# Encoder step on one core: each query tile in one transfer instead of two, differences of the weights ahead of scaling, row tiles normed ahead of stores

## The chip, the cores and the metric

The kernel runs on one core of one Trainium2 chip. The core has five engines with their own instruction streams: TensorE (PE, matmuls), VectorE (DVE), ScalarE (ACT), GpSimd (POOL) and SyncE (SP), which issues most of the DMAs here. Work is passed between them by semaphores. Sixteen DMA engines move the data. The metric is the time of one execution on the device in microseconds (us); a lower one is better.

## The reference, cut to what matters

One step of a two-layer encoder for 2048 prompt frames and 64 new frames (the sample), 16 heads of 64, model width 1024, in float32:

```python
def a_project(x, g, w_in):
    h = rms_norm(x, g)
    q, k, v, gate = jnp.split(h @ w_in, 4, axis=-1)
    return split_heads(q), split_heads(k), split_heads(v), gate
...
def band_attend(q, k, v, q_pos, k_pos, rel_bias):      # layer A: own chunk of 64 and 8 before it
    s = jnp.einsum('bqhd,bkhd->bhqk', q, k).astype(jnp.float32) * SCALE
    ...
    p = jax.nn.softmax(s, axis=-1).astype(v.dtype)
    return jnp.einsum('bhqk,bkhd->bqhd', p, v)
...
def sb_block(q, k, v, q_pos, k_pos):                   # layer B: stick-breaking, 128 queries
    z = jnp.einsum('bqhd,bkhd->bhqk', q, k).astype(jnp.float32) * SCALE
    mask = (k_pos[None, :] < q_pos[:, None])[None, None]
    log_fail = jnp.where(mask, jax.nn.log_sigmoid(-z), 0.0)
    later = jnp.flip(jnp.cumsum(jnp.flip(log_fail, -1), axis=-1), -1) - log_fail
    w = jnp.where(mask, jnp.exp(jax.nn.log_sigmoid(z) + later), 0.0)
    return jnp.einsum('bhqk,bkhd->bqhd', w.astype(v.dtype), v)
```

Layer A: norm, projection to q, k, v and gate, band attention, times SiLU(gate), output projection, residual. Then a shared projection to keys and values, and layer B: norm, projection to q and gate, stick-breaking attention over the shared keys and values, gate, output projection, residual, final norm.

## The kernel before

**Precision and planes.** Each float32 operand of a matmul is split into two parts: a rounded one, made by ACT, and the rest, made by DVE (`split`). The two parts are called planes, and lie beside each other in a tile (`[P, 2, CH]`, P = 128 partitions, CH = 512 frames). A product takes three matmuls.

**Stages on the time axis.** Projections of layer A to about 640 us of the span; band attention 640 to 1262, in two parts by `ORDER`, prompt blocks (1, 0) to 945 and then (3, 2); output projection to 1383; projections of layer B to 1955; stick-breaking attention 1955 to 3093, again in two parts (to 2300 and after it); the end of layer B to 3201. PE and most of the others work in an order that the program writes out; where the program says so (`order.on`), the instructions of the four engines stay in it.

**Scratch.** q, k, v, gates and the attention's outputs go through scratch in device memory, since they don't fit on chip. `lay[L]["q"][hp]` holds the queries of a pair of heads hp, both planes, one plane behind the other (`[2, P, T]`, T = 2112 frames). `put` writes a block of 512 frames of both planes, `load_q` (L1095) reads it for one head (64 of the 128 rows). The first 64 partitions of the tile `q` and the last 64 get the same 64 rows, since each plane of q meets both planes of the keys, which lie above each other in the tile `keys` or `kt`. So `load_q` issues two DMAs, each to 64 partitions, with rows of 2 KB for each plane. A tile q is 512 KB, the pool has three of them, and each item of the attention (one head, one block of 512 queries) uses one. There are 64 items in each layer, 32 in each part. `Queue.load` (L159) and `Queue.store` (L152) put all of these transfers into SP's one queue, which issues them in order. `Sample.queries` reads the 64 frames of the sample in the same scratch.

**Projections.** Each is made for two heads' pairs at a time (function `pair`), for the first 1024 frames (half 0) and then the last 1024 (half 1), in a scheme with seven products instead of eight, which needs sums and differences of blocks of the weights. `weights_of` makes steps for each pair's weights: `load`; `s1` and `s2` scale by the norm's weights (POOL, tile `wraw`, four instructions each); `b1`, `b2` split whole blocks; `-t1` to `-t4` take differences (POOL, `wraw<-wraw`); `t1` to `t4` split these (ACT and DVE, tile `t`). In `pair` the steps of this pair and the two after it (`this`, `following`, `third`) are placed by hand between the products of eight slots. The helper `times` gives three matmuls for each of four blocks; `plain(x)` copies a PSUM bank by ACT (tile `c`).

**Rows.** The values' loop takes row tiles of 128 frames: `fetched` loads one (`xt`), `normed` squares it on ACT (`junk`), makes `rstd` on POOL and scales it there, `turned` transposes it on PE (`ps_tr`), `parted` splits it. `leave()` copies, splits (`vs`, `vn`) and stores the values of a tile, and `tick()` runs waiting steps such as the conversion of the cached values (`vvp`).

Nearly all instructions of PE, ACT, DVE and POOL are recorded under one line, L115, that of the helper which pins the order; they are told apart by the names of their tiles.

Of the kernel before, what the change touches and what calls it, by code (L numbers as in the profile page):

```python
# [78 lines left out]
def f32(ap):  # L79
    return ap.bitcast(F32)  # L80
# [45 lines left out]
def encoder_step(ctx: ExitStack, tc: tile.TileContext, a: dict, o: dict):  # L126
# [73 lines left out]
    for L, rows in (("a", CACHE_A), ("b", PAST)):  # L200
        lay[L] = dict(


            q=[dram.tile([2, P, T], F32R, name=f"q_{L}{i}") for i in range(HP)],
            k=[dram.tile([2, P, T + rows], F32R, name=f"k_{L}{i}") for i in range(HP)],

            v=dram.tile([T + rows, H, P], F32R, name=f"v_{L}"),
            g=[dram.tile([P, T], F32, name=f"gate_{L}{i}") for i in range(HP)],

            o=[dram.tile([HP, P, CH if g < GROUPS else NS], F32, name=f"o_{L}{g}") for g in range(GROUPS + 1)],  # L210

            w={
                x: dram.tile([2, 2, P, 2, 4, P], F32R, name=f"w_{L}{x[0]}{x[1]}")
                for x in DEFER[L] if L in KEPT and x[1] % 2 == 0
            },
        )
# [47 lines left out]

    def put(L, kind, hp, cols, parts, by=nc.sync.dma_start):

        by(f32(lay[L][kind][hp][:, :, cols]).rearrange("s p t -> p s t"), f32(parts))


    def projections(L, x_of, begin, w_v, cv, gv, out_v, jobs, first, prompt, sample, stages):  # L270
        with ExitStack() as own, ExitStack() as beside, ExitStack() as early:
# [9 lines left out]
            def quarter(hf, k0, t0):  # L281
                return [lambda k, i=i: xs[hf][i][:, 4 * k0 + k, t0 * CH : t0 * CH + CH] for i in range(2)]
# [102 lines left out]
            def two_blocks(j, raw, home):  # L385

                out = []
                for i in range(2):
                    k = 2 * j + i
                    h_, l_ = home(k)  # L390
                    act.activation(h_, raw[:, i], AF.Copy, scale=gv[:, k : k + 1])
                    dve.scalar_tensor_tensor(l_, raw[:, i], gv[:, k : k + 1], f32(h_), ALU.mult, ALU.subtract)
                    out.append((h_, l_))
                return out

            def vw(pool):
                return lambda k: [pool.tile([P, CH], F32R, name=f"vw{x}", tag=f"vw{x}{k}", bufs=1) for x in "hl"]
# [132 lines left out]
            def run(does, *names):  # L530
                for x in names:
                    if x in does:
                        does.pop(x)()

            def times(ps, x, w, begin):
                if len(x[0](0).shape) > 2:
                    ps = ps.rearrange("p (r h c) -> p r h c", r=2, h=2)
                for k in range(4):
                    mm(ps, w[0](k), x[0](k), start=(begin and k == 0), stop=False, skip_group_check=True)
                    mm(ps, w[0](k), x[1](k), start=False, stop=False, skip_group_check=True)  # L540
                    mm(ps, w[1](k), x[0](k), start=False, stop=(k == 3), skip_group_check=True)

            def pair(hf, kind, c0, hp, forms, pools, this, following, third, event):
# [11 lines left out]
                def plain(ps):  # L555
                    c = cpool.tile([P, CH], F32, name="c", tag="c", bufs=CS[L])
                    act.activation(c, ps, AF.Copy)
                    return c
# [55 lines left out]
                def lagged():  # L614
                    while lagging:
                        lagging.pop(0)()

                x = psum.tile([P, CH], F32, name="ps_x", tag="mm", bufs=5)
                times(x, quarter(hf, 0, 0), w11, True)
                c1 = plain(x)  # L620
                run(this, "t2", "-t3")
                lagged()
                slot(0)
                z = psum.tile([P, CH], F32, name="ps_z", tag="mm", bufs=5)
# [29 lines left out]
                run(following, "b2")  # L654
                lagged()
                leave(0, 0, c1)
                run(third, "s1")
                slot(6)
                times(x, quarter(hf, 1, 1), t4, False)
                if kind == "k" and hf * HALF + CH - first >= 0:  # L660
                    x = plain(x)
                run(following, "-t2", "-t4")
                lagged()
                leave(0, 1, x)
                slot(7)
# [210 lines left out]
            with tc.tile_pool(name=f"v1_{L}", bufs=1) as pool, tc.tile_pool(name=f"v1s_{L}", bufs=1) as vspool:  # L876
                vps = two_places() if L == "b" else None

                class Strip:
                    def tile(self, shape, dtype, name, tag, bufs):  # L880
                        return opool.tile(shape, dtype, name=name, tag="ol", bufs=2)

                where = [(ahead, 2), (ahead, 2), (ahead, 2), (Strip(), 2), (ahead, 2), (ahead, 2), (pool, 1), (ahead, 2)]
                xt[3] = fetched(seq1[3], *where[3])
                for i, t in enumerate(seq1):
                    leave = values(1, 0, i, t, vws, vspool, vps)
                    tick()
                    if i + 4 < NK:
                        xt[i + 4] = fetched(seq1[i + 4], *where[i + 4])
                    if i + 2 < NK:  # L890
                        parted(seq1[i + 2], turned(seq1[i + 2], xt[i + 2]))
                    if i < 4:
                        values_beside(i, ("oh", "xr"))
                    if i == 5:
                        raw = [block_rows(1, j, ("xr", "xr", "oh", "oh")[j]) for j in range(4)]
                    if i == NK - 1:
                        vws = [x for j in range(4) for x in two_blocks(j, raw[j], vw(ahead if j < 2 else pool))]
                    tick()
                    leave()
                    if i + 3 < NK:  # L900
                        normed(seq1[i + 3], xt[i + 3], ahead)
                    if i == 3:
                        tmp = [opool.tile([P, 2, CH], F32, name="mixed", tag="ol", bufs=2) for _ in range(2)]
                        tmp = [x[:, j] for x in tmp for j in range(2)]
                        mixing = mix(1, 1, tmp)
                    if 3 <= i < NK - 2:
                        mixing.pop(0)()
                    tick()
                for i, t in enumerate(seq1):
                    leave = values(1, 1, i, t, vws, vspool, vps)  # L910
                    tick()
                    tick()
                    leave()
                    if i == 5:
                        run(made[0], "t1")
                    if i == 0:
                        assert not mixing
                        tmp = [ahead.tile([P, 2, CH], F32, name="mixed", tag="xt", bufs=2) for _ in range(2)]
                        tmp = [x[:, j] for x in tmp for j in range(2)]
                        mixing = [x for u in (2, 3, 0) for x in mix(1, u, tmp)]  # L920
                    for _ in range(1 + (i < 3)):
                        if mixing:
                            mixing.pop(0)()
                    if i == 0:
                        raws = [raw_tiles()]
                        new1 = slot(x_new.rearrange("p k t -> p (k t)"))
                        forms = [whole_forms("oh"), None, [new1]]
                        made = [weights_of(*todo[1][0], raws[0], forms)]
                        run(made[0], "load")
                    if i == 2:  # L930
                        run(made[0], "s1")
                    if i == 3:
                        run(made[0], "b1", "s2")
                    if i == 4:
                        run(made[0], "-t1")
                        forms[1] = whole_forms("ol")
                        run(made[0], "b2")
                    if i == 5:
                        assert not mixing
                        run(made[0], "-t2", "-t4")  # L940
                    tick()
                while waiting:
                    tick()
# [151 lines left out]
    def load_q(L, pool, hp, h, q0):  # L1095

        there(L, "q", hp, q0)
        q = pool.tile([P, 2, CH], F32R, name="q", tag="q", bufs=3)
        src = f32(lay[L]["q"][hp][:, h * DH : h * DH + DH, place(q0) : place(q0) + CH]).rearrange("s d t -> d s t")
        for x in range(2):  # L1100
            queue.load(f32(q[x * DH : x * DH + DH]), src)
        return q

    def load_gate(L, pool, hp, q0):
# [27 lines left out]
    class Sample:  # L1132
# [9 lines left out]
        def queries(self, hp):  # L1142
            q = self.q[hp % 3]
            for h in range(2):
                rows = slice(h * DH, h * DH + DH)
                src = f32(lay[self.L]["q"][hp][:, rows, NEW : NEW + NS])
                queue.load(f32(q[rows, :, rows]), src.rearrange("s d t -> d s t"))
            return q

        def gate(self, pool, hp):  # L1150
# [994 lines left out]
```

## Time and profile before

| | us |
|---|---|
| median of 3 runs (lowest, highest) | 3200.28 (3200.26, 3200.92) |
| the profiled execution's own time | 3202.8 |
| its span | 3201.0 |
| PE busy, of the span | 3132.4 |
| DVE, ACT, POOL busy | 2216.5, 1858.9, 1719.1 |
| mean granted PE clock | 0.998 |

The span is the time from the first to the last recorded instruction. Busy time counts only compute instructions. A row of the profile names the engine, the operation, the tile written and the tiles read (out<-in), the shapes, how many, and in brackets how long the engine had been idle before and what ended that. A row of the windows gives for a stretch of the span each engine's busy time and count, then PE's granted clock, the mean busy share of the 16 DMA engines and what they moved.

### The profile page before, as it was taken

How to read it: one execution, taken by the hardware profiler on the slowest of the kernel's cores; microseconds unless marked ns; L12 is line 12 of the kernel's file. 1: busy time of each engine (PE TensorE's matmuls, PEld its weight loads, DVE VectorE, ACT ScalarE, POOL GpSimd, SP SyncE). 2: the span in 40 equal slices, each digit the busy share in tenths (PEclk: the TensorE clock that was granted, in tenths of full speed). 3: DMA queues.
4: the chain of work that ended last, by engine and by line, in shares of the span. 5: the costliest groups of instructions: out<-in, count | busy, mean ns of one | idle time of the engine just before them, and what ended most of it. 6: DMA issues, size and time to landing. Idle time of an engine off the chain costs nothing.

```text
span 3201.0 us, 52147 instructions
## 1 busy us (share of the span) xinstructions
PE 3132.4 (98%) x16784; PEld 2614.5 (82%) x16784; DVE 2216.5 (69%) x3940; ACT 1858.9 (58%) x3743; POOL 1719.1 (54%) x2381
## 2 busy tenths in 40 slices
PE   9999999999999999999999999999999999999999
PEld 7888877778888998877888777888888878888877
DVE  5676466567778775257545664888877888888873
ACT  5444444468888775144544544666666666666652
POOL 3545367636565553035534372444567777777761
PEclk9999999999999999999999999999999999999999
DMA  6598448798899993477998768877644576445423
GB/s 228 199 327 306 170 165 286 247 258 229 227 271 265 250 239 132 155 241 250 324 322 313 269 240 262 234 215 208 191 118 140 155 228 176 115 136 143 133 74 122
DMA packets 476975, 685.28 MB, mean 214 GB/s; under 512 B 61169, under 2 KB 258321, under 8 KB 476702
## 3 DMA queue, kind: packets, MB, share of 16 engines
q1 hardware_dynamic: 474398, 673.56, 68.3%
q10 hardware_dynamic: 2304, 8.39, 0.7%
q8 instruction: 134, 2.20, 0.3%
q14 instruction: 139, 1.14, 0.1%
HBM read 423.06 MB, written 258.76 MB: 213 GB/s over the span
## 4 chain that ended last, share of the span: by engine, by line
PE 71%; DVE 10%; issue 6%; DMA 5%; POOL 4%; ACT 3%; SPq 0%; POOLq 0%; ACTq 0%; DVEq 0%
PE acc L115 11%; PE ps_x L115 10%; PE z L115 10%; PE wt L115 9%; PE ps_o L115 9%; PE ps_j L115 8%; PE ps_v L115 6%; PE ps_z L115 5%; DVE s L115 3%; PE ps_y L115 2%; DVE pl L115 2%; POOL wraw L115 1%; PE ps_q L115 1%; ACT ph L115 1%; DMA wraw<-in_w_in_a 1%
## 5 line engine op out<-in xcount | busy, mean ns | idle before, releaser
L115 DVE TENSOR_TENSOR pl<-wt,ph 128x512 fp32r<-128x512 f32 (+1 forms) x864 | 551.0, 653 | 109.7 <-ACT ph L115 106.0
L115 ACT ACTIVATE ph<-wt 128x512 fp32r<-128x512 f32 (+1 forms) x864 | 484.7, 577 | 191.8 <-PE wt L115 180.5
L115 PE MATMUL wt<-ident,s 128*128 128x128 f32 x3472 | 551.6, 274 | 9.1 <-DVE pl L115 6.4
L115 PEld LDWEIGHTS wt<-ident,s 128*128 128x128 f32 x3472 | 417.6, 141 | 84.2 <-DVE pl L115 13.3
L115 ACT ACTIVATE f<-z 128x512 f32<-128x512 f32 (+4 forms) x680 | 355.1, 536 | 192.5 <-PE z L115 131.7
L115 POOL TENSOR_TENSOR s<-f,s 128x256 f32<-128x256 f32 x416 | 360.3, 867 | 102.0 <-DVE s L115 93.9
L115 PE MATMUL acc<-ph,vt 128*128 128x512 f32 (+3 forms) x1088 | 374.6, 379 | 7.2 <-ACT ph L115 4.1
L115 PE MATMUL z<-kt,q 128*128 128x512 f32 (+3 forms) x1280 | 372.7, 378 | 4.2 <-ACT f L115 2.5
L115 PE MATMUL acc<-pl,vt 128*128 128x512 f32 (+3 forms) x1088 | 362.9, 367 | 8.7 <-DVE pl L115 8.2
L115 POOL TENSOR_TENSOR two<-f 128x256 f32<-128x256 f32 x416 | 259.1, 625 | 152.1 <-ACT f L115 137.0
L115 DVE TENSOR_TENSOR_SCAN s<-two,s,own 128x256 f32<-128x256 f32 x408 | 299.8, 737 | 34.5 <-POOL two L115 33.2
L115 POOL TENSOR_SCALAR s<-s,rc 128x640 f32<-128x640 f32 (+5 forms) x264 | 201.2, 768 | 223.1 <-DVE rc L115 161.1
L115 PEld LDWEIGHTS z<-kt,q 128*128 128x128 f32 x1280 | 220.0, 190 | 34.6 <-ACT f L115 9.3
L115 DVE CUSTOM_DVE_ANT_0 s<-z,bias 128x640 f32<-128x640 f32 (+4 forms) x256 | 184.4, 732 | 73.1 <-PE wt L115 54.2
L115 PEld LDWEIGHTS acc<-pl,vt 128*128 128x128 f32 x1088 | 193.7, 190 | 41.4 <-DVE pl L115 25.5
L115 PE MATMUL ps_x<-x_own,t 128*128 128x512 f32 x864 | 220.3, 403 | 6.8 <-DVE t L115 3.9
L115 DVE TENSOR_TENSOR_SCAN s<-f,own 128x128 f32<-128x128 f32 (+4 forms) x264 | 202.2, 787 | 29.7 <-ACT f L115 29.1
L115 PEld LDWEIGHTS acc<-ph,vt 128*128 128x128 f32 x1088 | 196.5, 190 | 30.2 <-ACT ph L115 9.1
L115 POOL TENSOR_TENSOR wraw<-wraw 128x512 f32<-128x512 f32 x96 | 140.1, 1469 | 138.5 <-DVE ohl L115 89.6
L115 PE MATMUL ps_o<-big,oh 128*128 128x512 f32 x544 | 213.7, 393 | 0.0
L115 PE MATMUL ps_o<-bigl,oh 128*128 128x512 f32 x544 | 213.0, 392 | 0.0
L115 ACT ACTIVATE s<-s,mn 128x640 f32<-128x640 f32 (+5 forms) x264 | 200.3, 760 | 18.1 <-DVE mn L115 16.9
(250 smaller groups left out, 7122.7 us busy)
## 6 DMA issues: line engine op xcount, KB each, us to landing
vt<-v_b SPq DMA_DIRECT2D x80, 512.0 KB, 4.9
v_b<-vs SPq DMA_DIRECT2D x64, 512.0 KB, 4.3
q<-q_a SPq DMA_DIRECT2D x128, 256.0 KB, 6.7
q<-q_b SPq DMA_DIRECT2D x128, 256.0 KB, 4.3
vt<-v_a SPq DMA_DIRECT2D x48, 512.0 KB, 8.4
kt<-k_b SPq DMA_DIRECT2D x96, 256.0 KB, 5.6
v_a<-vs SPq DMA_DIRECT2D x40, 512.0 KB, 3.4
keys<-k_a SPq DMA_DIRECT2D x80, 256.0 KB, 6.9
```

What stands on the lines that cost most here:

```text
L115: ins = op(*args, **kwargs)
```

## The change

Three edits.

1. The queries' scratch of a head pair becomes `[P, 2 * T]`: for each block of frames the two planes lie side by side, so that a row of a block of 512 frames is one run of 4 KB. `load_q` reads both planes of 64 rows in one DMA with the source given twice (a step of 0 and a count of 2 outermost), for all 128 partitions. `put` and `Sample.queries` go through the helper `both`, with the same number of transfers as before.
2. In `pair`, the split `t2` of this pair stands ahead of the copy `c1`; `-t3` stays behind it. The scaling `s1` of the pair after the next moves behind the next pair's differences `-t2` and `-t4`, from the place ahead of slot 6 to the end of its work.
3. In the values' loop of half 1, `normed` for row tile i + 3 moves ahead of `tick()` and `leave()`.

```diff
-            q=[dram.tile([2, P, T], F32R, name=f"q_{L}{i}") for i in range(HP)],
+            q=[dram.tile([P, 2 * T], F32R, name=f"q_{L}{i}") for i in range(HP)],
...
     def put(L, kind, hp, cols, parts, by=nc.sync.dma_start):
 
+        if kind == "q":
+            by(both(L, hp, cols), f32(parts))
+            return
         by(f32(lay[L][kind][hp][:, :, cols]).rearrange("s p t -> p s t"), f32(parts))
 
+    def both(L, hp, cols):
+
+        return f32(lay[L]["q"][hp][:, 2 * cols.start : 2 * cols.stop]).rearrange("p (s t) -> p s t", s=2)
...
                 times(x, quarter(hf, 0, 0), w11, True)
+                run(this, "t2")
                 c1 = plain(x)
-                run(this, "t2", "-t3")
+                run(this, "-t3")
                 lagged()
...
                 leave(0, 0, c1)
-                run(third, "s1")
                 slot(6)
...
                 run(following, "-t2", "-t4")
+                run(third, "s1")
                 lagged()
...
+                    if i + 3 < NK:
+                        normed(seq1[i + 3], xt[i + 3], ahead)
                     tick()
                     leave()
-                    if i + 3 < NK:
-                        normed(seq1[i + 3], xt[i + 3], ahead)
...
         q = pool.tile([P, 2, CH], F32R, name="q", tag="q", bufs=3)
-        src = f32(lay[L]["q"][hp][:, h * DH : h * DH + DH, place(q0) : place(q0) + CH]).rearrange("s d t -> d s t")
-        for x in range(2):
-            queue.load(f32(q[x * DH : x * DH + DH]), src)
+        src = f32(lay[L]["q"][hp][h * DH : h * DH + DH, 2 * place(q0) : 2 * (place(q0) + CH)])
+        twice = bass.AP(tensor=src.tensor, offset=src.offset, ap=[[0, 2], *src.ap])
+        queue.load(f32(q).rearrange("p s t -> p (s t)"), twice)
         return q
...
-                src = f32(lay[self.L]["q"][hp][:, rows, NEW : NEW + NS])
-                queue.load(f32(q[rows, :, rows]), src.rearrange("s d t -> d s t"))
+                queue.load(f32(q[rows, :, rows]), both(self.L, hp, slice(NEW, NEW + NS))[rows])
```

How the order of instructions changes, at the places that matter. First SP at the start of the band attention: `q` are the queries' tiles, `keys` and `vt` keys and values, `gate`, `bias` and `lraw` (weights for later) other transfers of the same queue. Before:

```order
L159 DMA q<-q_a_81 64x2x512 x2
L159 DMA keys<-k_a_89 64x2x512
L567 DMA gate_a_105<-hl 128x512
L159 DMA keys<-k_a_89 64x2x512 x3
L159 DMA bias<-bias_159 128x1280
L159 DMA vt<-v_a 128x4x256
L567 DMA gate_a_104<-hl 128x512
L159 DMA vt<-v_a 128x4x256
L567 DMA gate_a_104<-hl 128x512
L115 DMA lraw<-in_w_in_a 128x8x128
L159 DMA q<-q_a_81 64x2x512 x4
```

And now:

```order
L159 DMA q<-q_a_81 128x1x1024
L159 DMA keys<-k_a_89 64x2x512 x2
L574 DMA gate_a_105<-hl 128x512
L159 DMA keys<-k_a_89 64x2x512 x2
L159 DMA bias<-bias_159 128x1280
L159 DMA vt<-v_a 128x4x256 x2
L574 DMA gate_a_104<-hl 128x512
L115 DMA lraw<-in_w_in_a 128x8x128
L574 DMA gate_a_104<-hl 128x512
L159 DMA q<-q_a_81 128x1x1024 x2
```

Two loads of a tile q have become one of 128 rows of 1024 numbers; the others keep their order but for the stores of gates.

ACT in a pair of the projections of layer A, half 1: `t` is the split `t2`, `c` the copy of a PSUM bank. Before:

```order
L115 ACTIVATE vs<-vvp 128x8x64
L115 ACTIVATE c<-ps_x 128x512
L115 ACTIVATE t_4455<-wraw 128x512
L115 ACTIVATE hl<-ps_x 128x512
L115 ACTIVATE c<-ps_z 128x512
```

And now:

```order
L115 ACTIVATE vs<-vvp 128x8x64
L115 ACTIVATE hl<-c 128x512
L115 ACTIVATE t_4455<-wraw 128x512
L115 ACTIVATE c<-ps_x 128x512
L115 ACTIVATE hl<-ps_x 128x512
L115 ACTIVATE c<-ps_z 128x512
```

`t` and `c` have changed places.

POOL in the same place: `wraw<-wraw` are differences, `wraw<-wraw,g_a` the scaling, `vvp` the conversion of cached values. Before:

```order
L115 TENSOR_TENSOR wraw<-wraw 128x4x128
L115 TENSOR_SCALAR wraw<-wraw,g_a 128x256 x4
L115 TENSOR_TENSOR vvp<-vvp,vvr 128x512
L115 TENSOR_TENSOR wraw<-wraw 128x4x128 x3
L115 TENSOR_SCALAR wraw<-wraw,g_a 128x256 x4
```

And now:

```order
L115 TENSOR_TENSOR wraw<-wraw 128x4x128
L115 TENSOR_TENSOR vvp<-vvp,vvr 128x512
L115 TENSOR_TENSOR wraw<-wraw 128x4x128 x2
L115 TENSOR_SCALAR wraw<-wraw,g_a 128x256 x4
L115 TENSOR_TENSOR wraw<-wraw 128x4x128
L115 TENSOR_SCALAR wraw<-wraw,g_a 128x256 x4
```

Four scalings have moved behind two of the differences.

ACT in the values' loop of layer A, half 1: `vs` and `vn` are the values that leave, `junk` the square of the row tile. Before:

```order
L115 ACTIVATE big_177<-ps_tr 128x4x128 x2
L115 ACTIVATE vs<-vps 128x8x64
L115 ACTIVATE vs<-ps_v 128x8x64
L115 ACTIVATE vn<-ps_v 128x512
L115 ACTIVATE junk,ss<-xt 128x1024
L115 ACTIVATE x_own_174<-mixed 128x4x128
```

And now:

```order
L115 ACTIVATE big_177<-ps_tr 128x4x128 x2
L115 ACTIVATE junk,ss<-xt 128x1024
L115 ACTIVATE vs<-vps 128x8x64
L115 ACTIVATE vs<-ps_v 128x8x64
L115 ACTIVATE vn<-ps_v 128x512
L115 ACTIVATE x_own_174<-mixed 128x4x128
```

The square stands ahead of three activations that it stood behind.

## The prediction

> **What bounds the kernel now.** I read the page's head, the chain of work that ended last and the DMA queues first, then the PE's waits, then the stages one by one.
>
> ```profile
> span 3201.0 us, 52147 instructions
> PE 3132.4 (98%) x16784; PEld 2614.5 (82%) x16784; DVE 2216.5 (69%) x3940; ACT 1858.9 (58%) x3743; POOL 1719.1 (54%) x2381
> q1 hardware_dynamic: 474398, 673.56, 68.3%
> PE 71%; DVE 10%; issue 6%; DMA 5%; POOL 4%; ACT 3%; SPq 0%; POOLq 0%; ACTq 0%; DVEq 0%
> q<-q_a SPq DMA_DIRECT2D x128, 256.0 KB, 6.7
> q<-q_b SPq DMA_DIRECT2D x128, 256.0 KB, 4.3
> ```
>
> TensorE is busy for 3132.4 of 3201.0 us, so everything that an edit could give back is the idle remainder, 68.6 us. DMAs have 5% of the chain, and SP's own queue (SPq) 0%. The last two rows are the loads that the change rewrites: 256 of them, in 128 pairs, 256 KB each, landing 6.7 and 4.3 us after issue.
>
> The waits of the PE that the change can touch, of a list that is long and flat:
>
> ```profile
> PE z L115 <- DMA q<-q_a: 2.3, 1, 2.3
> PE ps_x L115 <- DVE t L115: 3.9, 6, 0.8
> PE ps_x L115 <- ACT t L115: 2.6, 1, 2.6
> PE ps_tr L115 <- POOL xt L115: 2.1, 3, 1.4
> PE acc L115 <- ACT ph L115: 4.1, 4, 3.0
> ```
>
> Columns: total us, times, longest. The queries' loads cost the PE one wait of 2.3 us in the whole program; their transfers are hidden. So a faster q load has 2.3 us to give, while a much slower one comes out from under its cover. Hence the stages that load queries, with the share and rate of the DMA engines (last two columns; PE's clock ahead of them):
>
> ```profile
> core 0: us, PE busy (x) PEld busy (x) DVE busy (x) ACT busy (x) POOL busy (x), PEclk, DMA share, GB/s
> 645.00:945.00 300.00, 288.07 (x1760) 253.57 (x1759) 217.20 (x632) 233.54 (x560) 165.03 (x194) 0.99 0.91 246
> 945.00:1240.00 295.00, 283.58 (x1875) 257.24 (x1873) 230.89 (x587) 234.10 (x513) 161.97 (x179) 1.00 0.91 239
> 1955.00:2300.00 345.00, 338.95 (x1977) 286.58 (x1977) 274.14 (x457) 210.62 (x449) 144.97 (x252) 1.00 0.81 227
> 2300.00:3093.00 793.00, 780.41 (x4446) 645.96 (x4445) 666.30 (x1069) 530.13 (x1055) 593.26 (x1095) 1.00 0.49 144
> 134.00:135.00 1.00, 1.00 (x6) 0.80 (x5) 0.83 (x2) 1.00 (x2) 0.00 (x0) 1.00 1.01 385
> 1262.00:1390.00 128.00, 126.94 (x570) 104.26 (x569) 37.04 (x61) 20.93 (x39) 3.90 (x5) 1.00 0.47 157
> ```
>
> The first two are the band attention's two parts (A1, A2), the next two the stick-breaking attention's (B1, B2). In A1 and A2 the DMA engines already work for 91% of the time. The last two windows give the speed of one of the 16 engines: 385 GB/s at share 1.01 is 23.8 GB/s each, 157 at 0.47 is 20.9.
>
> **The change part by part.**
>
> *The q load.* Removed: 128 issues on SP at 0.57 to 0.59 us, some 75 us of SP's time.
>
> ```profile
> L159 SPq DMA_DIRECT2D q<-q_a x128: 573/586/3514, 640.5 to 1212.5; - x128
> L159 SPq DMA_DIRECT2D q<-q_b x128: 573/593/1320, 1954.6 to 3028.3; - x128
> ```
>
> SPq has 0% of the chain, so I cost that at nothing. The bytes are the same, in rows of 4 KB instead of 2. What differs is the outermost step: the old transfers run over 64 rows, the new one says "twice" first, and then 64 rows. How does the hardware deal a transfer out to its engines? The trace has one case of a transfer without many rows, two loads of `vcur`, one of 16 rows of 4 KB and one of a single row of 4 KB (the window 1929.5 to 1933):
>
> ```profile
> DMA packets 34, 0.07 MB, mean 20 GB/s; under 512 B 17, under 2 KB 17, under 8 KB 34
> vcur<-v_raw SPq DMA_DIRECT2D x1, 64.0 KB, 2.0
> vcur<-v_raw SPq DMA_DIRECT2D x1, 4.0 KB
> ```
>
> No packet lies between 512 B and 2 KB: the sixteen rows went as 4 KB packets, whole, and the single row in some sixteen small ones of 256 B (4 KB by 16). So dealing goes by the outermost step that has more than one value: rows where there are rows, pieces of the row where there is one. The new load's outermost step has two values. By that reading each load goes as two halves of 256 KB, one on each of two engines. No load of before has a step of two outermost, so the price has two ends.
> - Spread over 16 engines as now: 524,288 B / 16 / 23.8 GB/s = 1.38 us of each engine for a q tile, as before; change nil.
> - On two engines: 262,144 B / 23.8 GB/s = 11.0 us of each of the two (12.5 us at 20.9).
>
> I take the second, as the `vcur` rows are nearest to it, and keep the first for a rival.
>
> [...]
>
> Now what two engines must carry. Each of the four parts loads 32 tiles (128 pairs by four): 32 x 11.0 = 352 us on those two. All other transfers still pass through the same two engines for their sixteenth, and queue behind 11 us pieces. From a part's share, the others' time on an engine is share x length - 32 x 1.38 = - 44 us; from its rate, (GB/s x length - 16.8 MB) / (16 x 23.8 GB/s), which leaves out the time that engines are slowed. I take the middle:
> - A1: 0.91 x 300 - 44 = 229 by share, (73.8 - 16.8) / 0.381 = 150 by rate; middle 190. 352 + 190 = 542 for 300 us: +242.
> - A2: 224 and 141, middle 183; 535 for 295: +240.
> - B1: 235 and 161, middle 198; 550 for 345: +205.
> - B2: 345 and 256, middle 300; 652 for 793: hidden, 0.
>
> Sum +687. The q pool has three buffers, so loads run up to two tiles ahead; that evens out bursts, but not a demand above what the engines carry. An item of A lasts 300 / 32 = 9.4 us, less than the 11 us that its q load alone needs. In B2 an item lasts 25 us, which covers 11.0 + 9.4. Behind a late q the PE's `z` waits, and then ACT, DVE and POOL one after the other; keys, values and gates are late with it, since they pass the same queue.
>
> *Pairs: t2 ahead.* `run(this, "t2")` moves before `c1`, s1 behind -t2 and -t4. The place in the trace (pairs, half 1, A):
>
> ```profile
> 522.39 3.81 POOL L115 TENSOR_SCALAR wraw<-wraw,g_a 128x256 f32<-128x256 f32 x4 [2.25 <-DMA wraw<-in_w_in_a]
> 525.70 0.60 ACT L115 ACTIVATE c<-ps_x 128x512 f32<-128x512 f32 x1 [3.05 <-PE ps_x L115]
> 526.17 4.36 POOL L115 TENSOR_TENSOR wraw<-wraw 128x512 f32<-128x512 f32 x3
> 527.49 0.63 ACT L115 ACTIVATE t<-wraw 128x512 fp32r<-128x512 f32 x1 [1.19 <-POOL wraw L115]
> ```
>
> The scaling of the third pair (3.81 us on POOL) stands ahead of the differences that `t` needs; ACT then waits 1.19 us for POOL, and the PE for DVE's `t`. With the scaling behind them, `t` is some 3.8 us earlier: the six waits of 3.9 us go. On ACT `c` (0.60 us) moves behind `t`, and what waits for `c`, the sum with `y` in slot 5, comes many matmuls later. The wait of 2.6 us has three ACT operations ahead of `t`, of which only `c` moves: -0.5. Scaling is now later by three differences of 1.45 us; it is for the pair after next, so nothing. Sum -4.4.
>
> *Row tiles normed sooner.* The square, `rstd` and scale of row tile i+3 stand ahead of the previous tile's stores instead of behind.
>
> ```profile
> 421.51 0.60 ACT L115 ACTIVATE vn<-ps_v 128x512 f32<-128x512 f32 x1 [1.16 <-DVE vs L115]
> 422.01 1.05 ACT L115 ACTIVATE junk<-xt 128x1024 bf16<-128x1024 f32 x1
> 424.44 1.20 POOL L115 TENSOR_SCALAR xt<-xt,rstd 128x1024 f32<-128x1024 f32 x1
> 425.70 1.09 PE L115 MATMUL ps_tr<-ident,xt 128*128 128x128 f32 x8 [1.42 <-POOL xt L115]
> ```
>
> ACT's square goes past three activations like `vn`, 0.60 us each, so 1.8 us earlier; the PE's 1.42 us goes, and I take 0.2 of the two shorter waits (2.1 in all): -1.6. The three activations are later by 1.05 us; `vs` then frees a PSUM bank later, of five; no wait for those shows.
>
> Sum of all: +687 - 6 = +681. The profiled execution took 3202.8 us (3201.0 of span and 1.8 around it), 2.5 above the runs' median of 3200.28. 3200.3 + 681 is about **3880**.
>
> **The rivals.**
>
> *The load spreads over 16 engines after all (faster).* The sums above give -6; issue and landing earlier take the wait of 2.3 us for q and part of the 3.0 us one for `ph`, since `ph` now stands on ACT ahead of an `sp` whose buffer waits for a key store: some 10 in all, 3190. For it: bytes and engines as before, longer rows. Against it: `vcur`. It decides from a dealing that does not go by the outermost step. Chance 0.07.
>
> *It spreads, and the small gains are lost to other waits*, as PE waits are many and short: 3194 to 3204, within 0.2% (6.4 us, about what a measurement of this kernel can tell from no change). Chance 0.05.
>
> *Two engines, but prefetch and slack hide more of it.* If only part of each stage pays, or the two engines change from load to load, A1 and A2 by the lower rows (502 and 493 us) cost 202 + 198, and B nothing: 3600. Without any delay of other transfers behind the pieces, A alone is 352 against 300 and 295: +109, 3310. For it: three buffers, and B2's slack. Against it: the shares of 0.91. Chance 0.15, most of it near 3600.
>
> *Two engines, and slower still.* At 12.5 us a tile and the others' time by share, A1 is 400 + 229 = 629, A2 624, B1 635: +329 +329 +290 = +948, 4145. And the PE's clock drops in long waits. After the 3.00 us gap that ends at 672.16 it shows:
>
> ```profile
> 672.16 0.80 PE L115 MATMUL acc<-ph,vt 128*128 128x512 f32 x1 [3.00 <-ACT ph L115]
> 673.00:676.00 3.00, 3.00 (x14) 2.70 (x13) 2.91 (x10) 2.15 (x6) 0.00 (x0) 0.50 1.09 261
> 676.00:679.00 3.00, 3.00 (x15) 2.82 (x15) 1.38 (x6) 1.68 (x6) 1.95 (x3) 0.58 1.07 343
> ```
>
> Clock 0.50 and then 0.58 for 3 us each is 1.5 + 1.3 = 2.8 us lost for a gap; at each of A's 64 items 180 us, 4325. But a PE that waits for DMAs has time to be slow in, so I leave it out of the sum. Chance 0.18.
>
> **How the numbers follow.** Two engines with the sum as it stands: 0.55, 3880, its own range 3700 to 4100. With the two cases beside it, slower has 0.88; faster 0.07, same 0.05. The range takes in the hidden case's upper part and the slow one's: 3550 to 4350, leaving out the 0.12 of the faster and the same and about 0.08 at its ends.
>
> **What would show it.** Issues of q in one row of 512 KB, 64 each for A and B, with landing at 11 us at least and far more where they queue (5 to 7 now). The wait `z` <- q, now 2.3 us, becomes the PE's longest by far, hundreds of us, in A1, A2 and B1; the DMA share falls in these stages, since 14 engines idle; B2 keeps its 793 us. The projections keep their lengths but for some 6 us, with the wait for `t` gone. The prediction is wrong if the q load lands in 5 to 8 us and stages A keep 300 and 295 us: then the load spreads. It is off in size if B2 lengthens too, since then bursts count and not means, or if PEclk in A falls well under 1.

## The result, and the profile after

| | before | changed |
|---|---|---|
| median, us (lowest to highest) | 3200.6 (3200.26 to 3206.27), 4 runs | 3919.78 (3911.69 to 3926.5), 4 runs |
| span of the profiled execution, us | 3201.0 | 3916.4 |
| PE busy, us | 3132.4 | 3298.6 |
| mean granted PE clock | 0.998 | 0.918 |

The ratio is 1.2237 (95% interval 1.2221 to 1.2252): 22% slower. The forecast was 3880, in a range of 3550 to 4350.

The same lines of the page as were shown of before: head, busy time, SP's DMA queue, the chain, and the queries' loads (the page gives no time to landing for any load of this queue now):

```profile
span 3916.4 us, 52050 instructions
PE 3298.6 (84%) x16784; PEld 2757.0 (70%) x16784; DVE 2226.6 (57%) x3940; ACT 1871.7 (48%) x3743; POOL 1711.9 (44%) x2381
q1 hardware_dynamic: 443934, 673.54, 53.0%
PE 35%; DMA 22%; DVE 4%; issue 4%; ACT 2%; SPq 1%; POOL 1%; ACTq 0%; POOLq 0%; DVEq 0%
q<-q_a SPq DMA_DIRECT2D x64, 512.0 KB
q<-q_b SPq DMA_DIRECT2D x64, 512.0 KB
```

The DMAs' part of the chain went from 5% to 22%, while the mean share of the 16 engines fell from 68.3 to 53.0%, for the same bytes: the DMA engines are less busy, and yet the program waits for them. The PE's longest waits of the changed kernel:

```profile
PE z L115 <- DMA q<-q_a: 242.8, 38, 13.3
PE z L115 <- DMA q<-q_b: 125.7, 17, 15.5
PE wt L115 <- POOL s L115: 67.0, 18, 12.9
PE z L115 <- issue: 36.4, 6, 14.1
```

The wait for q was 2.3 us in all. The PE runs the same 16784 matmuls in both kernels, in the same order but for 78 places at the start of the band attention, so that the start of the n-th matmul can be compared in the two traces. What a stage adds to the difference:

| stage (us of before) | forecast | changed kernel |
|---|---|---|
| up to the band attention (0 to 645) | -6 with the other projections | +2.1 |
| A1 (645 to 945) | +242 | +263.9 |
| A2 (945 to 1240) | +240 | +202.3 |
| output and B projections (1240 to 1955) | | -0.8 |
| B1 (1955 to 2300) | +205 | +197.2 |
| B2 (2300 to 3093) | 0 | +50.6 |
| the end | 0 | 0.0 |
| all | +681 | +715.4 |

The same four parts in the windows of the changed kernel, and behind them five microseconds in which little but one load of q was on its way (it was issued at 3742.92):

```profile
core 0: us, PE busy (x) PEld busy (x) DVE busy (x) ACT busy (x) POOL busy (x), PEclk, DMA share, GB/s
647.00:1211.00 564.00, 348.58 (x1760) 304.74 (x1759) 212.06 (x635) 237.72 (x560) 164.31 (x194) 0.77 0.42 127
1211.00:1708.00 497.00, 332.83 (x1871) 302.09 (x1871) 230.87 (x583) 236.97 (x513) 158.66 (x178) 0.82 0.49 146
2423.00:2965.00 542.00, 379.36 (x1976) 318.63 (x1975) 279.89 (x459) 214.92 (x451) 148.85 (x256) 0.85 0.46 142
2965.00:3808.00 843.00, 796.02 (x4441) 659.02 (x4442) 663.28 (x1066) 528.95 (x1052) 590.90 (x1090) 0.98 0.45 137
3745.00:3750.00 5.00, 4.68 (x27) 3.67 (x27) 4.94 (x9) 2.69 (x7) 4.18 (x9) 1.00 0.14 52
```

The last row is the mechanism by itself: a share of 0.14 is 2.2 of 16 engines, and 52 GB/s is 26 for each of two. By the trace's packet records this load is 128 packets of 4 KB, most of 159 ns (25.8 GB/s), the first begun at 3744.2 and the last ended at 3755.9: 11.7 us for one tile, where the forecast had 11.0. A load of keys came in between; 64 packets of 159 ns by themselves are 10.2 us.

SP was held up as well. Its rows at the start of A1 (start and length in us), first of before and then of the changed kernel:

```profile
654.95 3.87 SPq L159 DMA_DIRECT2D keys<-k_a  x4
```

```profile
665.35 3.05 SPq L159 DMA_DIRECT2D q<-q_a  x2
668.44 14.72 SPq L159 DMA_DIRECT2D keys<-k_a  x4
```

To issue four loads of keys behind two loads of q took 14.72 us instead of 3.87. Added up over the trace, SP's issues took 1104 us before and 2087 now, in A1 138 and 463. So what stands behind q in SP's queue is late already when it is issued.

### The profile page after: what moved, and what is told of

The parts are those of the page before. It is cut to its first block, busy times and chain, and to the rows that moved or that the text cites. A ratio compares the mean times of both kernels' runs of the same rounds, so it can differ in the third digit from the quotient of the medians.

```text
span 3916.4 us, 52050 instructions
## 1 busy us (share of the span) xinstructions
PE 3298.6 (84%) x16784; PEld 2757.0 (70%) x16784; DVE 2226.6 (57%) x3940; ACT 1871.7 (48%) x3743; POOL 1711.9 (44%) x2381
## 3 DMA queue, kind: packets, MB, share of 16 engines
q1 hardware_dynamic: 443934, 673.54, 53.0%
## 4 chain that ended last, share of the span: by engine, by line
PE 35%; DMA 22%; DVE 4%; issue 4%; ACT 2%; SPq 1%; POOL 1%; ACTq 0%; POOLq 0%; DVEq 0%
DMA q<-q_b 7%; PE ps_o L115 6%; PE acc L115 6%; PE z L115 6%; DMA q<-q_a 5%; PE wt L115 5%; PE ps_x L115 4%; DMA kt<-k_b 3%; PE ps_j L115 3%; PE ps_z L115 2%; PE ps_v L115 2%; DMA vt<-v_b 1%; DVE s L115 1%; PE ps_y L115 1%; DVE pl L115 1%
## 5 line engine op out<-in xcount | busy, mean ns | idle before, releaser
L115 PE MATMUL wt<-ident,s 128*128 128x128 f32 x3472 | 598.6, 290 | 76.7 <-POOL s L115 67.0
L115 PEld LDWEIGHTS wt<-ident,s 128*128 128x128 f32 x3472 | 453.2, 150 | 155.1 <-POOL s L115 72.8
L115 PE MATMUL z<-kt,q 128*128 128x512 f32 (+3 forms) x1280 | 389.5, 392 | 180.6 <-DMA q<-q_b 125.7
L115 PE MATMUL z<-keys,q 128*128 128x320 f32 (+4 forms) x896 | 223.1, 378 | 286.8 <-DMA q<-q_a 242.8
L115 PE MATMUL acc<-ph,vt 128*128 128x512 f32 (+3 forms) x1088 | 391.2, 395 | 14.4 <-ACT ph L115 9.1
L115 PE MATMUL acc<-pl,vt 128*128 128x512 f32 (+3 forms) x1088 | 381.4, 385 | 7.4 <-DVE pl L115 6.9
L115 PEld LDWEIGHTS z<-keys,q 128*128 128x128 f32 x896 | 170.2, 233 | 306.2 <-issue 275.4
L115 PEld LDWEIGHTS z<-kt,q 128*128 128x128 f32 x1280 | 229.1, 199 | 219.0 <-issue 166.5
L115 PEld LDWEIGHTS acc<-ph,vt 128*128 128x128 f32 x1088 | 210.6, 204 | 38.1 <-ACT ph L115 17.2
L115 PEld LDWEIGHTS acc<-pl,vt 128*128 128x128 f32 x1088 | 211.0, 207 | 37.2 <-DVE pl L115 22.4
```

Of the source, the lines that this page charges most:

```text
L115: ins = op(*args, **kwargs)
```

## The experiments

All are measured against the kernel before, on the same chip. Its median was 3203.39 us beside the runs with two loads, without the repetition and with 4 and 8 steps, and 3203.12 beside the others. Where it says "one run", the time is that of the profiled execution alone. The stages' differences are read as above.

**Undo the single transfer alone.** The changed kernel, with two transfers of 64 partitions from the new scratch.

```diff
-        twice = bass.AP(tensor=src.tensor, offset=src.offset, ap=[[0, 2], *src.ap])
-        queue.load(f32(q).rearrange("p s t -> p (s t)"), twice)
+        for x in range(2):
+            queue.load(f32(q[x * DH : x * DH + DH]).rearrange("p s t -> p (s t)"), src)
```

> The changed kernel, but a tile of queries is read by two transfers of 64 partitions each, from the new scratch with its rows of 4 KB; all else as in the change. If the loss comes from dealing by the outermost step (two values there, so two of 16 engines), it is gone: the attention parts take 300, 295, 345 and 793 us again, and the time is 3192 to 3202 (3200.3 less up to 6 for the moved instructions, if they give what the prediction says; the aligned traces show -1.7 us up to 482 us and +3.8 us in the pairs up to 645, which may be the moved scaling or the q loads that begin there). Rival, the new layout itself (4 KB rows, planes side by side) is slow: still above 3500. Rival, the moved instructions cost time: 3202 to 3206.

Measured: 3201.79 us, ratio 0.9998 (0.9989 to 1.0007), span 3198.1. Its windows are those of before:

```profile
645.00:945.00 300.00, 288.30 (x1772) 253.55 (x1772) 219.88 (x635) 235.13 (x563) 165.53 (x194) 0.99 0.89 248
945.00:1240.00 295.00, 285.10 (x1886) 258.87 (x1885) 231.54 (x591) 235.47 (x519) 163.04 (x183) 1.00 0.89 237
1955.00:2300.00 345.00, 339.06 (x1979) 287.03 (x1978) 274.42 (x457) 212.05 (x454) 146.56 (x255) 1.00 0.80 226
2300.00:3093.00 793.00, 780.06 (x4435) 645.57 (x4434) 665.92 (x1068) 526.67 (x1047) 593.80 (x1096) 1.00 0.49 144
```

The whole loss lies in the form of the load. The new scratch and the moved instructions together are not to be told from no change: the aligned span is 2.9 us shorter, within the interval.

**Keep the step of two, drop the repetition.** The outermost step reads two different blocks of queries, so one half of each tile holds another block's queries.

```diff
-        twice = bass.AP(tensor=src.tensor, offset=src.offset, ap=[[0, 2], *src.ap])
-        queue.load(f32(q).rearrange("p s t -> p (s t)"), twice)
+        low = f32(lay[L]["q"][hp][h * DH : h * DH + DH, 2 * place(q0 - q0 % (2 * CH)) : 2 * (place(q0 - q0 % (2 * CH)) + CH)])
+        other = bass.AP(tensor=low.tensor, offset=low.offset, ap=[[2 * CH, 2], *low.ap])
+        queue.load(f32(q).rearrange("p s t -> p (s t)"), other)
```

> The changed kernel, but the outermost step of two reads two different blocks of queries (the item's and its neighbour's) instead of the same one twice, so the lower or upper 64 partitions hold another block's queries. Dealing by the outermost step: still two values outermost, so two engines, and the time stays at 3920, within 40. Rival, reading the same rows twice in one transfer is what is slow: near 3200.

Measured: 3917.24 us (one run); A1 +264.9, A2 +199.4, B1 +197.8, B2 +53.1, each within 4 us of the changed kernel. Reading the same rows twice is not what costs.

**Two transfers again, but dealt by 2, 4 and 8 steps.** Only the order of rows within a head differs from the run with two loads, for 4:

```diff
+        (step, n), run = src.ap
+        dealt = bass.AP(tensor=src.tensor, offset=src.offset, ap=[[step, 4], [4 * step, n // 4], run])
         for x in range(2):
-            queue.load(f32(q[x * DH : x * DH + DH]).rearrange("p s t -> p (s t)"), src)
+            queue.load(f32(q[x * DH : x * DH + DH]).rearrange("p s t -> p (s t)"), dealt)
```

> As the run dealt to four, but two outermost steps of one row, then 32 of two rows: two transfers of 64 partitions a tile, 128 KB on each of two engines per transfer; the queries' rows are permuted. Dealing by the outermost step: the same 11.7 us of two engines for a tile as in the changed kernel, so 3900 to 3940 although the transfers are two, of 256 KB, without a repetition. Rival, the single transfer of 512 KB over 128 partitions adds its own cost: clearly below 3900.

> The changed kernel, but two transfers of 64 partitions a tile, each with its rows taken in another order (outermost four steps of one row, then 16 of four rows), so the queries' rows of a head are permuted. Bytes, row length and number of transfers are those of the run with two loads. Dealing by the outermost step: four engines, 5.5 us of each for a tile, 32 x 5.5 = 176 us a part; with the others' time of the prediction A1 366 for 300, A2 359 for 295, B1 374 for 345, B2 nothing: +159, about 3360 (3280 to 3450). Rival, what is slow is the 512 KB transfer over 128 partitions, or its repetition: 3200.

> As the run with four outermost steps, but eight, then eight of eight rows; the queries' rows are permuted. Dealing by the outermost step: eight engines, 2.75 us of each a tile, 88 us a part; with the others' 190, 183 and 198 it is 278 for 300, 271 for 295, 286 for 345: all hidden by the means, 3200, up to 3260 where bursts count. Rival, two transfers that aren't dealt at all: 3200 as well; only beside the run with four does this one tell.

Measured, one run each (us):

| outermost steps | time | A1 | A2 | B1 | B2 |
|---|---|---|---|---|---|
| 2 | 3930.68 | +261.0 | +202.2 | +203.3 | +59.8 |
| 4 | 3468.82 | +103.2 | +87.8 | +52.3 | +24.3 |
| 8 | 3277.30 | +22.2 | +35.7 | +11.2 | +5.2 |
| 64 (two loads) | 3201.79 | -1.1 | -1.5 | +1.4 | +0.4 |

With two steps the loss is whole although there are two transfers of 256 KB and no repetition, so neither the size of the transfer nor its 128 partitions carries it. From 2 to 8 steps it falls as the number of engines rises.

The pages let the engines be counted. SP's queue (packets, MB, share) in the run with two loads, then with 2, 4 and 8 steps:

```profile
q1 hardware_dynamic: 447774, 673.56, 67.7%
q1 hardware_dynamic: 444190, 673.54, 53.5%
q1 hardware_dynamic: 444702, 673.54, 63.2%
q1 hardware_dynamic: 445726, 673.55, 68.6%
```

Against the first row 3584, 3072 and 2048 packets are missing, which is 256 loads by 14, by 12 and by 8; in the changed kernel (443934) it is 3840, 256 by 16 less 128 by 2. In the packet records these are all packets of 4 bytes, and the packets with data are the same in number. Each run fits one small packet for each engine of each load exactly, with 2, 4, 8 and 16 engines; that such a packet stands for an engine is inferred from this fit.

But two of the three expectations missed: four steps came out at 3469, above the stated 3280 to 3450, and eight at 3277, above its 3260. The windows say where, first for four (A1 and B1), then for eight (A1 and A2):

```profile
645.00:1048.00 403.00, 320.57 (x1759) 279.13 (x1758) 212.35 (x631) 235.79 (x560) 163.32 (x194) 0.87 0.65 180
2144.00:2542.00 398.00, 350.66 (x1982) 295.38 (x1981) 277.65 (x459) 213.87 (x451) 145.63 (x253) 0.96 0.69 195
```

```profile
646.00:968.00 322.00, 298.01 (x1757) 260.75 (x1757) 216.21 (x632) 233.93 (x560) 163.79 (x193) 0.96 0.86 224
968.00:1299.00 331.00, 294.15 (x1878) 268.09 (x1877) 231.95 (x587) 235.02 (x515) 160.21 (x179) 0.95 0.86 219
```

Take from each share the mean of the q loads over 16 engines (32 x 11.7 x 2 / 16 = 47 us), and what is left is the other transfers' time on one engine. For A1 it is 0.42 x 564 - 47 = 190 us with two engines, 0.65 x 403 - 47 = 215 with four, 0.86 x 322 - 47 = 230 with eight. Add what a busy engine has of q, 374, 187 and 94 us: 564, 402 and 324, against stages of 564, 403 and 322. The other rows shown give 415 for B1's 398 and 332 for A2's 331. The reckoning takes 11.7 us for a tile in every run, though in A1 the packets of 4 KB, most of them q's, took 183, 217 and 246 ns on average; part of what it counts as the others' growth is q's own. The packet records say it without a sum: with two steps (the changed kernel) at least two packets are in flight in all but 2 of A1's 564 us, and exactly two in 299 of them; with four steps at least four in all but 10 of 403, and with eight at least eight in all but 15 of 322. So A1 lasts about as long as its most loaded engines are busy. By this reckoning the middle of 190 was right for the case that was forecast and too low for the other two.

**One transfer, dealt to sixteen.** The scratch holds each head's rows twice, so a tile is 128 rows one behind the other; a block is written by four stores instead of one.

```diff
-            q=[dram.tile([P, 2 * T], F32R, name=f"q_{L}{i}") for i in range(HP)],
+            q=[dram.tile([2 * P, 2 * T], F32R, name=f"q_{L}{i}") for i in range(HP)],
...
-            by(both(L, hp, cols), f32(parts))
+            for h in range(2):
+                for x in range(2):
+                    by(both(L, hp, cols)[h * P + x * DH : h * P + x * DH + DH], f32(parts)[h * DH : h * DH + DH])
...
-        src = f32(lay[L]["q"][hp][h * DH : h * DH + DH, 2 * place(q0) : 2 * (place(q0) + CH)])
-        twice = bass.AP(tensor=src.tensor, offset=src.offset, ap=[[0, 2], *src.ap])
-        queue.load(f32(q).rearrange("p s t -> p (s t)"), twice)
+        src = f32(lay[L]["q"][hp][h * P : h * P + P, 2 * place(q0) : 2 * (place(q0) + CH)])
+        queue.load(f32(q).rearrange("p s t -> p (s t)"), src)
...
```

> The changed kernel, but the scratch of queries holds each head's 64 rows twice, one copy behind the other, so a tile is one transfer of 128 rows without a repeated step; a block of queries is written by four stores of 64 partitions instead of one of 128. Dealing by the outermost step: 128 rows, sixteen engines, so the loss is gone: 3195 to 3215 (64 blocks by 3 more stores at about 0.6 us are 115 us of SP's time, and 32 MB more written is 88 us of all engines, beside other work). What one transfer instead of two is worth shows against the run with two loads: nothing, since the PE waits there for no q; the stores may cost some us in the first attention, where the engines are busy for 0.89 of the time. Rival, one transfer over 128 partitions is slow by itself: above 3500.

Measured: 3310.51 us, ratio 1.0338 (1.0324 to 1.0352). The load does what it should: A1 -5.7, A2 -1.7, B1 -0.5, B2 +5.1 (about the run with two loads). Its queue's 459806 packets fit sixteen small ones for each load: the 447774 of the run with two loads, less 128 loads by 16, plus 80 blocks by 3 more stores by 16 and by 128 more rows. The loss, over 100 us and not expected, is nearly all in the projections, in the pairs of half 0 (+43.4) and half 1 (+30.2) of layer A, and in B (+22.5 from 1515 to 1770 and +15.6 from 1770 to 1870). The q loads and the stores of q of this kernel, the stores of before, and the PE's first two waits:

```profile
L159 SPq DMA_DIRECT2D q<-q_a x64: 319/325/2959, 712.7 to 1276.6; - x64
L270 SPq DMA_DIRECT2D q_a<-hl x128: 446/988/2048, 227.7 to 643.0; - x128
```

```profile
L267 SPq DMA_DIRECT2D q_a<-hl x32: 359/384/1537, 224.1 to 571.5; - x32
```

```profile
PE ps_c L115 <- DMA kr<-in_cache_b_k: 50.1, 4, 19.2
PE ps_x L115 <- ACT hl L115: 27.2, 5, 9.6
```

(Times in the first three rows are shortest, median and longest on SP, in ns.) A block's stores took 0.384 us of SP and now take four times 0.988, 4.0 us, and the loads of cached keys `kr` stand behind them in the same queue. The load of `kr` that SP issued at 227.62 in the kernel before is issued at 250.11 here, behind rows like this one, in which twelve stores take 11.22 us:

```profile
227.72 11.22 SPq L270 DMA_DIRECT2D q_a<-hl  x12
```

These loads land as fast as before (median 4.8 us after issue in both kernels), so they are late because they are issued late. How much of the stores' time comes from their shape and how much from the bytes written twice, no run separates. SP had 0% of the chain before; that said nothing of what ten times the issue time of these stores would do.

**The pairs' edit alone, and the row tiles' edit alone**, each made in the kernel before.

```diff
+                run(this, "t2")
                 c1 = plain(x)
-                run(this, "t2", "-t3")
+                run(this, "-t3")
...
-                run(third, "s1")
...
                 run(following, "-t2", "-t4")
+                run(third, "s1")
```

> The kernel before with the pairs' edit alone (t2 ahead of the copy, s1 behind the differences). By the prediction -4.4 us of span, all of it in the pairs of half 1 (482 to 645 and 1871 to 1955). By the profile of the run with two loads, where the waits for t have turned into waits of ps_x for ACT's hl and c, nothing there: within 1.5 us of before in these stretches.

Measured: 3201.89 us (one run), span 3200.1. From 482 to 645 the difference is +1.4, from 1870 to 1955 +0.3. The PE's waits in the pairs of half 1 of layer A, before and then with the edit (482 to 646):

```profile
PE ps_x L115 <- DVE t L115: 3.9, 6, 0.8
PE ps_x L115 <- ACT hl L115: 0.3, 1, 0.3
```

```profile
PE ps_x L115 <- ACT hl L115: 4.1, 6, 1.7
PE ps_x L115 <- DVE t L115: 0.7, 2, 0.4
```

The wait for `t` went from 3.9 to 0.7 us, as forecast, and the one for `hl` grew by 3.8. In the longest of them ACT stands in a split that waits for POOL:

```profile
600.54 0.63 ACT L115 ACTIVATE x_new<-wraw 128x512 fp32r<-128x512 f32 x1 [2.26 <-POOL wraw L115]
601.07 0.61 ACT L115 ACTIVATE hl<-c 128x512 f32<-128x512 f32 x1
601.80 0.47 PE L115 MATMUL ps_x<-big,t 128*128 128x512 f32 x1 [1.68 <-ACT hl L115]
```

The activations `hl`, which the next products wait for, are behind it in ACT's order. This split (tile `x_new`) is `t1` of the next pair, which the edit doesn't move. In the kernel before ACT waits at the same place for POOL, and longer:

```profile
601.41 0.63 ACT L115 ACTIVATE x_new<-wraw 128x512 fp32r<-128x512 f32 x1 [3.03 <-POOL wraw L115]
```

There the PE came to the product only at 602.67 and found `hl` done (it started at 601.95 and takes 0.62 us). With the edit the PE is ready 2.6 us sooner, and this split only 0.9 us.

```diff
+                    if i + 3 < NK:
+                        normed(seq1[i + 3], xt[i + 3], ahead)
                     tick()
                     leave()
-                    if i + 3 < NK:
-                        normed(seq1[i + 3], xt[i + 3], ahead)
```

> The kernel before with the row tiles' edit alone. By the prediction -1.6 us: the wait of ps_tr for POOL's xt at 425.70, 1.42 us, is gone, and half of the one at 1433.72. By the run with two loads the first is gone, and the second still there with 0.45; -1.3 in the stretch from 386 to 482, nothing elsewhere.

Measured: 3203.67 us (one run), span 3201.9. From 386 to 482 it gives -0.7. The three waits of `ps_tr` for POOL's `xt`, 2.1 us before, are one of 0.5, the 1.42 at 425.70 among those gone; and the waits of `ps_v` for ACT's `vwh` are longer:

```profile
PE ps_tr L115 <- POOL xt L115: 0.5, 1, 0.5
PE ps_v L115 <- ACT vwh L115: 3.8, 3, 2.0
```

They were 1.2 us before. The longest, 2.04 us at 1441.30, lies in the projections of layer B, where the stretch from 1390 to 1515 is longer by 1.7; whether the edit makes it is not shown, as the same stretch moved by -1.4 in the run with the pairs' edit alone, which changes nothing there. Neither edit changes the time by what can be told here, and no run is faster than the kernel before by more than its spread.

## Why the prediction was right

**The dealing.** It is borne out by each run: two steps outermost, and two engines carry the load (0.14 of 16, 52 GB/s in the changed kernel), whether it is one transfer or two, repeated or not (3919.8 us as changed, 3917.2 without the repetition, 3930.7 as two); four and eight steps cost less (3468.8 and 3277.3 us), 64 or 128 nothing that can be told in the attention (1.5 and 5.7 us a part at most). But its source, the packets of two `vcur` loads, was misread. The row counts 34 packets, 17 of them under 512 B, so 17 are of 2 KB or more: the sixteen rows and the single row, each whole. The 17 small ones have 4 bytes each in the packet records; no pieces of 256 B are there. Counted as above, 16 + 1 small packets are sixteen engines for sixteen rows and one for the single row, which was not dealt out in pieces. So these loads showed rows that go whole, and no step of two; that the conclusion drawn from them came out right was partly luck, and the runs are what shows it. One transfer instead of two halves brought nothing here that can be told: as loads of 128 rows it changed the attention's parts by 6 us at most, and the repeated form added 715.

**The sum.** A tile took 11.7 us of each engine in the company of other loads, not 11.0, and the others' time in A1 was about the 190 taken. A1, A2 and B1 came to 663 where 687 was forecast: A2 was 38 us too high, B1 8 too high and A1 22 too low. With B2's 51, which was forecast as nothing, the errors cancel in part, so that 3880 came so near to 3919.8 is partly luck. By the reckoning above A2 would be 0.49 x 497 - 47 + 374 = 571, 74 more than it lasted, and B1 0.46 x 542 - 47 + 374 = 576, 34 more; packets that overlap on an engine count double in a share (the shares of 1.07 and 1.09 in the prediction's rows show it), and q loads issued ahead fall into the part before, so the reckoning is off by 15 and 6% there. The packet records agree with the limit there too: at least two packets are in flight in all but 5 us of A2 and 2 us of B1.

**The step that failed: B2 at nothing.** It cost 50.6 us. Its mean demand is no limit: 0.45 x 843 - 47 + 374 = 706 us of 843. So the mean over a part was the wrong measure where loads come in bunches; the prediction had named a longer B2 as the sign of that. Some of the PE's waits in B2 of the changed kernel:

```profile
PE z L115 <- DMA kt<-k_b: 11.3, 3, 6.4
PE acc L115 <- ACT ph L115: 9.1, 4, 7.0
PE z L115 <- DMA vt<-v_b: 6.5, 1, 6.5
PE z L115 <- DMA q<-q_b: 5.2, 1, 5.2
```

Keys and values are late as well as q. The prediction expected that, since they pass the same queue, and the trace bears it out where it was read. Four loads of keys behind a load of q, first of before and then of now, with the PE's wait that follows:

```profile
2797.40 2.55 SPq L159 DMA_DIRECT2D kt<-k_b  x4
```

```profile
3495.72 10.67 SPq L159 DMA_DIRECT2D kt<-k_b  x4
3514.25 1.19 PE L115 MATMUL z<-kt,q 128*128 128x512 f32 x2 [6.38 <-DMA kt<-k_b]
3336.78 0.38 ACT L115 ACTIVATE ph<-wt 128x256 fp32r<-128x256 f32 x1 [8.22 <-DMA q<-q_b]
```

The last row is behind the longest wait for `ph`, 7.0 us: by the profile, ACT itself had waited for a load of q. The other waits in B2 were not followed back. B2's loss falls to 24.3 and 5.2 with four and eight engines, as it would.

**The small edits: -6 forecast, nothing to be told.** In the pairs the wait named was removed and its place taken by another. The prediction asked what became later by the move (`c`, the scaling) and not what the PE would meet next if it came sooner: in the longest of the new waits, activations on ACT behind a split of the next pair, which came sooner by 0.9 us where the PE came sooner by 2.6. The 2.6 us wait of `ps_x` for `t`, taken to shrink by 0.5, stayed as one of 2.5 for `c`.

**The rivals.** That the load spreads is refuted by the 5 us window (0.14 of 16); that prefetch hides more, by A1's 564 us for 374 + 190. That rival's 3600 has B at nothing, though by its own lower row B1 would have been 352 + 161 = 513 for 345; B1 cost 197. The slow case was priced too high: a tile took 11.7 us and not 12.5, and while the clock did fall in the parts with the long waits (PEclk 0.77 in A1 and 0.82 in A2, for 0.99 and 1.00 before), PE busy rose by 61 us in A1 and 49 in A2, where 180 was priced. That even this is hidden behind the loads is argued from A1's length, and not shown.

**The same two engines.** The forecast's 352 us a part stand on the same two engines for each load, and the others' time beside it on a sixteenth of every other transfer there; no row of before shows either, and the trace doesn't number the DMA engines. But 374 us of q fill A1 only if they fall on the same engines, since spread evenly they would be 47, and one window shows it: the two loads of q in the row at 665.35 were both issued by 668.40, and in the next microseconds about two engines work and not four (0.15 of 16, 58 GB/s; exactly two packets in flight in 3.64 of the 5 us):

```profile
669.00:674.00 5.00, 3.88 (x13) 3.21 (x14) 3.74 (x13) 3.95 (x9) 0.00 (x0) 0.61 0.15 58
```

The sixteenth shows in a load of keys issued at 3749.00, behind the load of q of 3742.92: of its 256 packets of 2 KB 224 had begun by 3752.49, which is the part of fourteen engines, and the other 32 began from 3755.52 on, as the last of q's ended. Which two of the sixteen they are stays open.

## What to carry to other kernels

Before two transfers are merged into one, look at the outermost step (here it was the source's): where it was 2, the transfer ran on two DMA engines (0.14 of 16, 11.7 us for 512 KB) although it filled 64 or 128 partitions, and loads behind it in SP's queue were issued late (four of keys in 14.72 us for 3.87). Cost such a load as its bytes on the busiest engine, and add the other transfers' share there; where this exceeded a stage's length, the stage took about that long (A1 564 us for 300, where the forecast's sum had 542), and where it came near it, bursts cost too (B2 +50.6 at 706 of 843). A share of the chain of 0% says that a queue is not late now, not that it can take ten times the work (a block's stores at 4.0 us of SP for 0.384 went with 100 us of loss).

## What the runs showed of the hardware that was not expected

SP's time to issue a load of q, medians for layer A and then B: 0.586 and 0.593 us for the halves in rows of 2 KB before, 0.626 and 0.531 for the repeated load of 512 KB, 0.486 and 0.587 for a half in one run of 4 KB a row, 0.325 and 0.332 for 128 rows in one transfer. A store over 64 partitions took 0.988 us where one of twice the size, over 128, took 0.384. Half of the partitions was not half of the price, but more; the shortest of each were 0.446 and 0.359, so part of the 0.988 may be the fuller queue and not the shape. For one shape the two layers' medians differ by up to a fifth, so that of the loads only the 128 rows stand apart clearly.
